# Both heads of a pair alternate on the two halves of the rows in the products inside the chunks of an RWKV-7 layer

## The chip, the cores and the metric

One core of a Trainium2 chip runs the whole kernel. The metric is device time in microseconds: the median of several runs of one program. Three runs of the kernel before are shown, and one more execution was profiled.

## What is computed

A diffusion-backbone layer over 2048 latent tokens with a context prefix of 256 tokens, width 1024, all in float32. After a modulated norm one projection feeds two groups of eight heads: attention in a 2-D neighbourhood, and RWKV-7 time mixing in both directions. Both are joined by an output projection, and a SwiGLU follows. The part that the change touches is the recurrence:

```python
# per direction and head, state S of 64 x 64, one step for each token
sa = einsum('bhvk,bhk->bhv', s, a_t)
s = s * w_t[:, :, None, :] + sa[..., None] * b_t[:, :, None, :] + v_t[..., None] * k_t[:, :, None, :]
y = einsum('bhvk,bhk->bhv', s, r_t)
# context tokens first (256), then the latent tokens (2048); forwards and backwards; 8 heads
```

## The kernel before

The program has three stages. `phase1` computes the norm, the input projection, and the decayed vectors of the recurrence, which it writes to the tensor `d_b`. `phase2` runs the recurrence and the attention beside each other. `phase4` makes the output projection and the SwiGLU.

The recurrence is computed in chunks of 64 tokens. There are 18 steps `s` (2 of the context and 16 of the latent tokens, 128 tokens each, so 2 chunks per step), 4 pairs of heads `hp` and 2 directions. In `phase2` it is made of four kinds of streams:

- `build(s, hp, w)`, 72 times (lines 965 to 1011): the products inside a step's chunks, for one pair of heads. For each of the pair's two heads `h` it multiplies, for four (direction, chunk) indices `j`, a 64x128 block of `bk` by a 64x128 block of `u.ga` (64x64 for the two steps of the context). Head 0's operands stand in partitions 0 to 63, head 1's in 64 to 127, so a product uses half of the rows of TensorE's array. Each head has a PSUM bank of its own, taken when its turn comes: four matmuls on line 996, then two ACT copies of the triangular part into `lx` (line 1002; one for each half of 32 rows, into columns that the inversion wants), a masked DVE product into `ga` (line 1004) and another into `gb` (line 1008), then the bank goes back.
- `inverses()`, 9 times, each for two steps (lines 1036 to 1111): the inverse of the triangular matrices `lx`. DVE transposes (line 1047), POOL masks, DVE solves 32x32 blocks by some 30 operations on the tile `lu` (lines 1061 to 1074), transposes back (lines 1077 and 1079), and small matmuls on lines 1094 and 1103 make the off-diagonal blocks, with copies between (1099, 1107).
- `lates(g)`: transposes of `bk` for the state's update (line 1029). It takes a bank too.
- `chains(g)`, for two groups of two pairs: the recurrence over the 36 chunks, where each chunk needs the state of the chunk before. A chunk of one group is eight matmuls on each of lines 1174, 1182 and 1189 with copies between them, and the outputs on lines 1200 and 1203.

Beside them stand the attention's streams (`prepare`, two `head` streams, `products`): matmuls on lines 672, 751, 754, 759, 789, 791, 824 and 830.

Only two PSUM banks, `bank0` and `bank1`, are shared by builds, lates, inverses and the attention's `prepare`. A stream asks for one by `yield "get", z, 1` and gives it back by `put`. The builds of two steps write the buffer `lx`, of which there are two; so the builds of the last two steps wait until the chain has passed step 13, and the chain's last two steps (four chunks) wait for the ninth inverse, which waits for all eight of those builds.

The order of the program is made by `emit`: a planner that holds the streams as generators, with a cost for each piece (`yield "run", ("PE", 1.0)` and the like), and takes the stream that can start first by its costs. A scheduler of the framework then sets the final order on each engine's queue. Each queue is served in order. [...]

The lines of the build before that matter:

```python
for h in range(2):
    z = []
    yield "get", z, 1
    yield "run", ("PE", 1.0)
    gp = z[0].rearrange("p (j t) -> p j t", j=4)
    for j in range(4):
        nc.tensor.matmul(gp[:, j, 0:N], bk[H[h], j], u.ga[H[h], h:3:2 - h, j, :] if s > 1 else
                         u.ga[H[h], h, j, :], start=True, stop=True)
```

Of the kernel before, what the change touches and what calls it, by code (L numbers as in the profile page):

```python
# [3 lines left out]

# [1 line left out]

# [7 lines left out]
AF = mybir.ActivationFunctionType  # L14
# [28 lines left out]

class K:
    pass


def setup(k, ctx, tc, I):
# [857 lines left out]
def phase2(k):  # L906
# [3 lines left out]
    tc, nc, I = k.tc, k.nc, k.I  # L910
    with ExitStack() as ctx:
# [10 lines left out]
        H = (slice(0, 64), slice(64, 128))  # L922
# [30 lines left out]
        for i in range(NU):  # L953
            u = K()
# [10 lines left out]
        def build(s, hp, w):  # L965

            G, j0 = s // 2, 4 * (s % 2)
# [19 lines left out]


            N = 128 if s > 1 else 64
            for h in range(2):  # L990
                z = []
                yield "get", z, 1
                yield "run", ("PE", 1.0)
                gp = z[0].rearrange("p (j t) -> p j t", j=4)
                for j in range(4):
                    nc.tensor.matmul(gp[:, j, 0:N], bk[H[h], j], u.ga[H[h], h:3:2 - h, j, :] if s > 1 else  # L996
                                     u.ga[H[h], h, j, :], start=True, stop=True)
                yield "run", ("ACT", -0.43), ("DVE", -0.34)
                ko = H[1 - h]
                for i in range(2):  # L1000
                    p0 = slice(64 * h + 32 * i, 64 * h + 32 * i + 32)
                    nc.scalar.activation(lx[p0, hp, j0:j0 + 4, 0:64 - 32 * i], gp[p0, :, 32 * i:64], AF.Copy)
                dc = "p (d c) t -> p d c t"
                nc.vector.tensor_tensor(u.ga[ko, h].rearrange(dc, d=2), gp[ko, :, 0:64].rearrange(dc, d=2),
                                        maskS[ko, :, None, :].to_broadcast([64, 2, 2, 64]), op=ALU.mult)
                if s > 1:
                    yield "run", ("DVE", -0.34)
                    nc.vector.tensor_tensor(u.gb[:, h].rearrange(dc, d=2), gp[:, :, 64:128].rearrange(dc, d=2),  # L1008
                                            maskI[:, h, :, None, :].to_broadcast([P, 2, 2, 64]), op=ALU.mult)
                yield "put", z[0]  # L1010
            yield "post", ("built", s, hp)

        def lates(g):
# [22 lines left out]
        def inverses():  # L1036
# [3 lines left out]
            for s in range(NS // 2):  # L1040
                yield ("wait",) + tuple(("built", 2 * s + e, hp) for e in range(2) for hp in range(4))
                lx = LX[s]
                lu = lx.rearrange("p g j t -> p (g j) t")
                lv = lu[:, :, 0:32]
                x = cp.tile([P, 32, 32], F32, tag="lu", name="lu")
                yield "run", ("DVE", 1.2)
                nc.vector.transpose(x.rearrange("u s t -> u t s"), lv.rearrange("s u t -> s t u"))
# [654 lines left out]
```

## Time and profile before

| | |
|---|---|
| median of 3 runs | 3642.16 us (3630.34 to 3642.43) |
| the profiled execution | 3625.81 us, span 3624.1 us, mean granted clock 0.972 |
| PE busy (matmuls) | 3497.2 us, 96% of the span |
| DVE, ACT, POOL busy | 69%, 43%, 29% |
| recurrence and attention (`phase2`) on PE | 889 to 1998 us of the span |
| line 996 | 1152 records, 177.85 us of busy time |

The profiled execution is 16 us (0.45%) shorter than the median of the runs. Busy time counts a matmul from its start to its modelled end; the matmuls overlap in the array, so the time that one takes from the others is read from the distance between starts. The granted clock is the share of TensorE's full clock (2.4 GHz); 0.5 is its lower level, 1.2 GHz.

### The profile page before, as it was taken

How to read it: one execution, taken by the hardware profiler on the slowest of the kernel's cores; microseconds unless marked ns; L12 is line 12 of the kernel's file. 1: busy time of each engine (PE TensorE's matmuls, PEld its weight loads, DVE VectorE, ACT ScalarE, POOL GpSimd, SP SyncE). 2: the span in 40 equal slices, each digit the busy share in tenths (PEclk: the TensorE clock that was granted, in tenths of full speed). 3: DMA queues.
4: the chain of work that ended last, by engine and by line, in shares of the span. 5: the costliest groups of instructions: out<-in, count | busy, mean ns of one | idle time of the engine just before them, and what ended most of it. 6: DMA issues, size and time to landing. Idle time of an engine off the chain costs nothing. (4 is left out here: it accounts for less than half of the span.)

```text
span 3624.1 us, 67102 instructions
## 1 busy us (share of the span) xinstructions
PE 3497.2 (96%) x25330; PEld 2916.3 (80%) x25330; DVE 2505.1 (69%) x4780; ACT 1541.8 (43%) x3502; POOL 1060.5 (29%) x1011
## 2 busy tenths in 40 slices
PE   7899999999999999999999999999899999899999
PEld 5787878889667777767776787888799999799998
DVE  7758886772686666676785674344877778777776
ACT  4524343442555555455555444323433333333332
POOL 3425543552000000000010342333433334433332
PEclk9999999999899999999999999999999999999999
DMA  7546666555443343433434455333412222422222
GB/s 240 164 147 200 194 193 182 162 162 124 127 89 108 109 90 106 129 67 93 131 99 142 151 189 180 97 93 98 149 59 70 70 70 70 163 67 70 70 70 67
DMA packets 502339, 440.70 MB, mean 122 GB/s; under 512 B 106096, under 2 KB 424960, under 8 KB 502016
## 3 DMA queue, kind: packets, MB, share of 16 engines
q1 hardware_dynamic: 502016, 436.42, 41.3%
q8 instruction: 199, 3.26, 0.4%
q14 instruction: 124, 1.02, 0.1%
HBM read 328.54 MB, written 107.75 MB: 120 GB/s over the span
## 5 line engine op out<-in xcount | busy, mean ns | idle before, releaser
L1311 ACT ACTIVATE w<-raw 128x512 fp32r<-128x512 f32 x440 | 269.8, 627 | 496.1 <-PE acc L1600 186.9
L1520 PE MATMUL acc<-ua,w 128*128 128x384 f32 x2464 | 469.9, 336 | 6.9 <-POOL w L1312 3.3
L1600 PE MATMUL acc<-w,fh 128*128 128x512 f32 x1408 | 437.8, 396 | 19.5 <-ACT fh L1311 7.6
L1312 DVE TENSOR_TENSOR w<-raw,w 128x512 fp32r<-128x512 f32 x308 | 277.5, 904 | 247.4 <-ACT w L1311 122.7
L1520 PEld LDWEIGHTS acc<-ua,w 128*128 128x128 f32 x2464 | 433.2, 189 | 10.9 <-POOL w L1312 4.6
L209 PE MATMUL acc<-u,wh 128*128 128x512 f32 (+3 forms) x1120 | 347.1, 390 | 11.2 <-DVE sh L247 6.1
L1600 PEld LDWEIGHTS acc<-w,fh 128*128 128x128 f32 x1408 | 267.8, 191 | 80.4 <-ACT fh L1311 9.2
L493 PE MATMUL acc<-wt,u 128*128 128x256 f32 x2496 | 320.1, 287 | 4.8 <-DVE sh L247 2.2
L493 PEld LDWEIGHTS acc<-wt,u 128*128 128x128 f32 x2496 | 306.9, 193 | 12.0 <-issue 4.3
L1591 POOL TENSOR_TENSOR raw<-raw,gate 128x512 f32<-128x512 f32 x132 | 181.4, 1384 | 413.4 <-DMA raw<-in_w_dram 364.0
L1600 PE MATMUL acc<-w,fl 128*128 128x512 f32 x704 | 270.1, 393 | 0.0
L1312 POOL TENSOR_TENSOR w<-raw,w 128x512 fp32r<-128x512 f32 x132 | 185.8, 1408 | 275.3 <-PE acc L1520 59.1
L1520 PE MATMUL acc<-ux,w 128*128 128x384 f32 x1232 | 252.1, 335 | 0.6 <-DVE w L1312 0.4
L209 PEld LDWEIGHTS acc<-u,wh 128*128 128x128 f32 (+1 forms) x1120 | 205.8, 191 | 57.7 <-issue 10.8
L1502 PE MATMUL acc<-ua,w 128*128 128x512 f32 x1056 | 241.7, 389 | 2.3 <-POOL w L1312 1.4
L1502 PEld LDWEIGHTS acc<-ua,w 128*128 128x128 f32 x1056 | 198.0, 188 | 44.0 <-POOL w L1312 1.9
L209 PE MATMUL acc<-u,wl 128*128 128x512 f32 (+3 forms) x560 | 217.4, 388 | 3.6 <-DVE wl L200 3.5
L1520 PEld LDWEIGHTS acc<-ux,w 128*128 128x128 f32 x1232 | 216.7, 188 | 2.1 <-DVE w L1312 1.2
L1605 DVE TENSOR_TENSOR h<-h,acc 128x512 f32<-128x512 f32 x192 | 126.2, 682 | 99.6 <-PE acc L1600 99.2
L996 PE MATMUL bank<-ga,bk 64*128 64x128 f32 (+1 forms) x1152 | 177.8, 302 | 1.4 <-DVE gb L1008 0.6
L1512 DVE TENSOR_TENSOR t<-acc,t 128x384 f32<-128x384 f32 x308 | 169.4, 550 | 14.0 <-PE acc L1520 7.4
L1312 POOL TENSOR_TENSOR w<-s,w 128x512 fp32r<-128x512 f32 x88 | 130.7, 1486 | 149.6 <-PE acc L1520 59.2
(257 smaller groups left out, 7092.3 us busy)
## 6 DMA issues: line engine op xcount, KB each, us to landing
raw<-in_w_dram SPq DMA_DIRECT2D x132, 512.0 KB
raw<-in_w_dram SPq DMA_DIRECT2D x132, 256.0 KB
wada<-in_w_ada_dram SPq DMA_DIRECT2D x96, 256.0 KB
d_b<-bk SPq DMA_DIRECT2D x72, 256.0 KB
bkl<-d_b SPq DMA_DIRECT2D x144, 128.0 KB
bk<-d_b SPq DMA_DIRECT2D x72, 256.0 KB
d_b<-ar SPq DMA_DIRECT2D x136, 128.0 KB
xt<-in_x_dram SPq DMA_DIRECT2D x32, 512.0 KB
```

The source lines that it names most:

```text
L209: nc.tensor.matmul(acc[:m, :n], a_[:, kk % 4, :m], b_[b][:, kk, :], start=(i == 0), stop=(i == 23))
L493: nc.tensor.matmul(acc[:, 256 * e:256 * e + 256], a_[b][:, kk, (j + e) * P:(j + e + 1) * P], ws[kk][:, h, :], start=(i == 0), stop=(i == 23))
L996: nc.tensor.matmul(gp[:, j, 0:N], bk[H[h], j], u.ga[H[h], h:3:2 - h, j, :] if s > 1 else u.ga[H[h], h, j, :], start=True, stop=True)
L1311: nc.scalar.activation(hl[0], v, AF.Copy)
L1312: eng.tensor_tensor(hl[1], v, hl[0].bitcast(F32), op=sub)
L1502: nc.tensor.matmul(acc, hl[wi][:, kk, :], u[ui][:, 4 * hf + kk, :], start=q == 0, stop=q == 23)
L1512: vadd = lambda o, x, y: nc.vector.tensor_tensor(o, x, y, op=add)
L1520: nc.tensor.matmul(acc, w[wi][:, kk, :], u[i][ui][:, kk, :], start=q == 0, stop=q == 11)
L1591: nc.gpsimd.tensor_tensor(raw, raw, g2[:, o], op=ALU.mult)
L1600: nc.tensor.matmul(acc, a_[:, f, ts], w2[f][:, hl, :], start=(i == 0), stop=(i == 6 * np_ - 1))
L1605: nc.vector.tensor_tensor(hs[j][:, o], hs[j][:, o], acc, op=add)
```

## The change

Both heads of a pair now take their banks at the same time (`get` of 2), and the eight matmuls of a build are issued in the order head 0, head 1, head 0, head 1, over `j`. A small class chains them (`issue_after`), so that the scheduler keeps this order. The planner's cost of the matmuls is 1.0 once for both heads, where it was 1.0 for each. The two ACT copies of a head become one copy of 64 rows x 256 into `lx`, and the shift of the lower 32 rows by 32 columns, which the second copy had made, is now done by two POOL copies of 32 rows x 1024 at the head of each inverse. Each bank is given back when its own head's copies are planned.

```diff
+class Run:
+    def __init__(s, k):
+        s.k, s.last = k, None
+    def next(s):
+        return s.k.tc.issue_after(s.last) if s.last else nullcontext()
...
             N = 128 if s > 1 else 64
+            z = []
+            yield "get", z, 2
+            yield "run", ("PE", 1.0)
+            gp = [v.rearrange("p (j t) -> p j t", j=4) for v in z]
+            run = Run(k)
+            for j in range(4):
+                for h in range(2):
+                    with run.next():
+                        run.last = nc.tensor.matmul(gp[h][:, j, 0:N], bk[H[h], j], u.ga[H[h], h:3:2 - h, j, :] if s > 1
+                                                    else u.ga[H[h], h, j, :], start=True, stop=True).ins
+            dc = "p (d c) t -> p d c t"
             for h in range(2):
-                z = []
-                yield "get", z, 1
-                yield "run", ("PE", 1.0)
-                gp = z[0].rearrange("p (j t) -> p j t", j=4)
-                for j in range(4):
-                    nc.tensor.matmul(gp[:, j, 0:N], bk[H[h], j], u.ga[H[h], h:3:2 - h, j, :] if s > 1 else
-                                     u.ga[H[h], h, j, :], start=True, stop=True)
-                yield "run", ("ACT", -0.43), ("DVE", -0.34)
+                yield "run", ("ACT", -0.45), ("DVE", -0.34)
                 ko = H[1 - h]
-                for i in range(2):
-                    p0 = slice(64 * h + 32 * i, 64 * h + 32 * i + 32)
-                    nc.scalar.activation(lx[p0, hp, j0:j0 + 4, 0:64 - 32 * i], gp[p0, :, 32 * i:64], AF.Copy)
+                nc.scalar.activation(lx[H[h], hp, j0:j0 + 4, :], gp[h][H[h], :, 0:64], AF.Copy)
...
-                yield "put", z[0]
+                yield "put", z[h]
...
                 lv = lu[:, :, 0:32]
+                for h in range(2):
+                    p0 = slice(64 * h + 32, 64 * h + 64)
+                    nc.gpsimd.tensor_copy(lu[p0, :, 0:32], lu[p0, :, 32:64])
                 x = cp.tile([P, 32, 32], F32, tag="lu", name="lu")
```

How the order moves is seen at two places on PE's queue. The first is two builds of an early step, among the attention's matmuls (`sw`, `sx`, `po`), before:

```order
L996 MATMUL bank_9727<-ga_9773,bk 128x128 x4
L759 MATMUL sx<-kc,qz_9809 128x256
L789 MATMUL sx<-ident,pr 128x128 x2
L996 MATMUL bank_9728<-ga_9771,bk 128x128 x4
L791 MATMUL sw_9781<-ident,pr 128x128 x3
L830 MATMUL po<-ident,oT 128x128
L996 MATMUL bank_9727<-ga_9773,bk 128x128 x4
L751 MATMUL sw_9781<-ks,qz_9810 128x512
L754 MATMUL sw_9781<-mk 128x512
L824 MATMUL po<-pr,vc 64x128
L996 MATMUL bank_9728<-ga_9771,bk 128x128 x4
```

and one of these builds now (line 996 has become line 1008 of the new file):

```order
L1008 MATMUL bank_9727<-ga_9773,bk 128x128
L761 MATMUL sw_9781<-ks,qz_9810 128x512
L764 MATMUL sw_9781<-mk 128x512
L1008 MATMUL bank_9728<-ga_9773,bk 128x128
L1008 MATMUL bank_9727<-ga_9773,bk 128x128
L1008 MATMUL bank_9728<-ga_9773,bk 128x128
L1008 MATMUL bank_9727<-ga_9773,bk 128x128
L1008 MATMUL bank_9728<-ga_9773,bk 128x128
L1008 MATMUL bank_9727<-ga_9773,bk 128x128
L1008 MATMUL bank_9728<-ga_9773,bk 128x128
```

The build's two blocks of four have become one matmul, other work, and seven alternating ones. 52 of the 72 builds are cut in this way, after the first matmul, and 7 in another; 13 stand whole.

The second place is the ninth, last inverse (`bank<-x1t,lx` and `bank<-lx,fs`). Before, the rows around its first matmuls were these:

```order
L830 MATMUL po<-ident,oT 128x128
L1189 MATMUL pch_9729<-zv,tt 64x64 x2
L751 MATMUL sw_9781<-ks,qz_9808 128x512
L754 MATMUL sw_9781<-mk 128x512
L1094 MATMUL bank_9728<-x1t,lx 32x32 x32
L1094 MATMUL bank_9727<-x1t,lx 32x32 x32
L1182 MATMUL pch_9730<-rs,lx 64x64 x8
L1200 MATMUL pch_9729<-z_20374,ga_9767 64x64 x2
```

Now they are these (1275 and 1412 are `phase4`'s lines 1261 and 1398, 1108 and 1117 are the inverse's 1094 and 1103, 1196 and 1040 are 1182 of the chain and 1029 of the lates):

```order
L1008 MATMUL bank_9727<-ga_9755,bk 128x128
L1412 MATMUL mtp<-ident,mx 128x128 x4
L1275 MATMUL g<-gup,gd 128x512
L1412 MATMUL mtp<-ident,mx 128x128 x8
L1275 MATMUL g<-gup,gd 128x512 x3
L1108 MATMUL bank_9728<-x1t,lx 32x32 x32
L1108 MATMUL bank_9727<-x1t,lx 32x32 x32
L1117 MATMUL bank_9728<-lx,fs 32x32 x32
L1117 MATMUL bank_9727<-lx,fs 32x32 x32
L1196 MATMUL pch_9729<-rs,lx 64x64 x8
L1040 MATMUL bank_9728<-ident,bkl 128x128 x4
```

Attention stood on both sides of the last inverse; it no longer does. The attention's last matmul on PE (line 830 before) had 133 matmuls of `phase2` behind it, and now has 881. Those are, in the order now: 63 of the builds' (8 builds but one matmul), 120 on each of the chain's three lines (15 chunks of one group), 128 on each of the two lines of the outputs (16 such chunks), 44 of the lates' transposes, and the 128 of the last inverse; with 24 and 6 matmuls of `phase4` between them.

## Rows read from the trace of the kernel before

**Rows 1.** The page's first part: busy time of each engine, share of the span, instructions.

```profile
PE 3497.2 (96%) x25330; PEld 2916.3 (80%) x25330; DVE 2505.1 (69%) x4780; ACT 1541.8 (43%) x3502; POOL 1060.5 (29%) x1011
```

**Rows 2.** Stretches of the span: from and to, length, then busy time of PE, PEld, DVE, ACT and POOL (with instructions), the granted clock, the DMA's share and GB/s.

```profile
889.00:1970.00 1081.00, 1052.44 (x12037) 774.31 (x12036) 737.56 (x1863) 585.44 (x1638) 53.85 (x65) 0.95 0.41 106
1970.00:1998.00 28.00, 20.22 (x262) 15.18 (x260) 21.26 (x41) 9.98 (x22) 6.61 (x4) 0.76 0.76 203
1420.00:1466.00 46.00, 43.09 (x585) 35.88 (x584) 17.49 (x44) 19.36 (x49) 4.26 (x10) 0.67 0.31 89
1435.00:1466.00 31.00, 31.00 (x292) 26.13 (x286) 9.58 (x24) 10.70 (x28) 0.00 (x0) 0.50 0.22 65
```

**Rows 3.** The stretch of `phase2`, instructions of line 996 alone: busy time of PE and PEld, granted clock, DMA.

```profile
889.00:1998.00 1109.00, 177.85 (x1152) 148.94 (x1152) 0.94 0.42 108
```

**Rows 4.** PE's timeline: start and length in us, engine, line, operation, out<-in, shapes, records merged. A head's four matmuls and the row after them, then one matmul alone and the row after it.

```profile
1200.71 1.16 PE L996 MATMUL bank<-ga,bk 64*128 64x128 f32 x8
1201.80 0.91 PE L751 MATMUL sw<-ks,qz 128*128 128x384 f32 x2
...
1347.23 0.49 PE L996 MATMUL bank<-ga,bk 64*128 64x128 f32 x2
1347.64 1.13 PE L751 MATMUL sw<-ks,qz 128*128 128x512 f32 x2
```

**Rows 5.** PE's timeline at two more places. First the attention's products, whose two heads alternate on the two halves of the columns (22 records from 1331.76 to 1333.22), and behind them eight matmuls of two builds: four of a head 1 and four of a head 0, so of different halves of the rows. Then, at 1584, eight matmuls of two builds that are both of a head 0, so of the same half.

```profile
1331.76 0.54 PE L824 MATMUL po<-pr,vc 128*64 128x128 f32 x5
...
1333.22 1.71 PE L996 MATMUL bank<-ga,bk 64*128 64x128 f32 x16
1334.86 0.45 PE L1189 MATMUL pch<-zv,tt 128*64 128x64 f32 x6
...
1584.10 2.05 PE L996 MATMUL bank<-ga,bk 64*128 64x128 f32 x16
1586.08 0.33 PE L1182 MATMUL pch<-rs,lx 64*64 64x64 f32 x4
```

**Rows 6.** Who waited for whom on PE in 889 to 1998: engine, tile, line, what ended the wait; us in total, times, longest. The rows of line 996.

```profile
PE bank L996 <- DVE gb L1008: 0.6, 1, 0.6
PE bank L996 <- DVE ga L1004: 0.4, 1, 0.4
```

**Rows 7.** Groups of instructions by line and shape, in 889 to 1998 (the POOL row: of the whole span): busy us, mean ns of one, then idle time before them and what ended it.

```profile
L1002 ACT ACTIVATE lx<-bank 32x256 f32<-32x256 f32 x144 | 53.6, 373 | 116.2 <-PE bank L996 109.8 <-DVE z L1194 1.5 <-DVE z L1206 1.3
L1002 ACT ACTIVATE lx<-bank 32x128 f32<-32x128 f32 x144 | 38.7, 268 | 1.7
L1210 ACT COPY zv<-pch 64x256 f32<-64x256 f32 x128 | 46.7, 365 | 65.8 <-PE pch L1203 57.3 <-issue 4.9 <-DVE ot L834 2.2
L1004 DVE TENSOR_TENSOR ga<-bank,maskS 64x256 f32<-64x256 f32 x144 | 60.5, 420 | 151.4 <-ACT lx L1002 150.1
L329 POOL COPY sq<-rho 128x512 f32<-128x512 f32 x16 | 11.3, 706 | 0.6
```

**Rows 8.** PE's timeline near the end of `phase2`, at the full clock: two of the chain's pieces, `phase4`'s transposes, and the first and the last row of one chunk's outputs (lines 1200 and 1203, from 1970.65 to 1972.76).

```profile
1967.23 0.68 PE L1182 MATMUL pch<-rs,lx 64*64 64x64 f32 x16
1967.84 0.69 PE L1189 MATMUL pch<-zv,tt 128*64 128x64 f32 x16
...
1969.42 0.82 PE L1398 MATMUL mtp<-ident,mx 128*128 128x128 f32 x6
...
1970.65 0.33 PE L1200 MATMUL pch<-z,ga 64*64 64x64 f32 x4 [0.30 <-DVE z L1194]
...
1972.76 1.13 PE L1261 MATMUL g<-gup,gd 128*128 128x512 f32 x2
```

**Rows 9.** PE's timeline inside 1435 to 1466, where no attention stands on PE: the chain's pieces, a head of a build, an output piece, and the lates' transposes.

```profile
1436.02 1.12 PE L1189 MATMUL pch<-zv,tt 128*64 128x64 f32 x16
1437.07 0.47 PE L1182 MATMUL pch<-rs,lx 64*64 64x64 f32 x2
1437.48 2.07 PE L996 MATMUL bank<-ga,bk 64*128 64x128 f32 x8
...
1440.74 0.48 PE L1203 MATMUL pch<-zv,gb 128*64 128x64 f32 x4
...
1463.27 1.12 PE L1029 MATMUL bank<-ident,bkl 128*128 128x128 f32 x4
```

**Rows 10.** The last inverse on DVE: its first transpose, its last, and its last copy (timeline); then the busy time of DVE and POOL on the tile `lu` in that stretch, and the reductions, which write another tile.

```profile
1836.11 2.14 DVE L1047 STREAM_TRANSPOSE lu<-lx 128x1024 f32<-128x1024 f32 x1
...
1893.11 1.90 DVE L1079 STREAM_TRANSPOSE x1t<-lu 128x1024 f32<-128x1024 f32 x1
...
1911.24 0.69 DVE L1107 COPY lx<-bank 32x512 f32<-32x512 f32 x1
...
1836.00:1896.00 60.00, 24.37 (x30) 1.26 (x1) 1.00 0.45 123
...
L1073 DVE TENSOR_REDUCE red<-xtmp 128x112 f32<-128x448 f32 (+3 forms) x7 | 6.7, 951 | 0.1
```

More of the change, by code (lines that the diff above doesn't have):

```diff
@@ L2 @@
 import math
-from contextlib import ExitStack
+from contextlib import ExitStack, nullcontext
 import numpy as np
@@ L989, in build @@
             N = 128 if s > 1 else 64
-            for h in range(2):
-                z = []
-                yield "get", z, 1
-                yield "run", ("PE", 1.0)
-                gp = z[0].rearrange("p (j t) -> p j t", j=4)
-                for j in range(4):
-                    nc.tensor.matmul(gp[:, j, 0:N], bk[H[h], j], u.ga[H[h], h:3:2 - h, j, :] if s > 1 else
-                                     u.ga[H[h], h, j, :], start=True, stop=True)
-                yield "run", ("ACT", -0.43), ("DVE", -0.34)
-                ko = H[1 - h]
-                for i in range(2):
-                    p0 = slice(64 * h + 32 * i, 64 * h + 32 * i + 32)
-                    nc.scalar.activation(lx[p0, hp, j0:j0 + 4, 0:64 - 32 * i], gp[p0, :, 32 * i:64], AF.Copy)
-                dc = "p (d c) t -> p d c t"
-                nc.vector.tensor_tensor(u.ga[ko, h].rearrange(dc, d=2), gp[ko, :, 0:64].rearrange(dc, d=2),
+            z = []
[9 more added lines that the diff above has]
+            dc = "p (d c) t -> p d c t"
+            for h in range(2):
+                yield "run", ("ACT", -0.45), ("DVE", -0.34)
+                ko = H[1 - h]
+                nc.scalar.activation(lx[H[h], hp, j0:j0 + 4, :], gp[h][H[h], :, 0:64], AF.Copy)
+                nc.vector.tensor_tensor(u.ga[ko, h].rearrange(dc, d=2), gp[h][ko, :, 0:64].rearrange(dc, d=2),
                                         maskS[ko, :, None, :].to_broadcast([64, 2, 2, 64]), op=ALU.mult)
@@ L1007, in build @@
                     yield "run", ("DVE", -0.34)
-                    nc.vector.tensor_tensor(u.gb[:, h].rearrange(dc, d=2), gp[:, :, 64:128].rearrange(dc, d=2),
+                    nc.vector.tensor_tensor(u.gb[:, h].rearrange(dc, d=2), gp[h][:, :, 64:128].rearrange(dc, d=2),
                                             maskI[:, h, :, None, :].to_broadcast([P, 2, 2, 64]), op=ALU.mult)
-                yield "put", z[0]
+                yield "put", z[h]
             yield "post", ("built", s, hp)
```

## The prediction

> **What bounds the kernel now.** I read the page's busy shares first: PE is busy 96% of the span, the next engine, DVE, 69% [rows 1]. The change touches `phase2` alone, so I looked at its stretches next. From 889 to 1970 us, where recurrence and attention stand beside each other, PE is busy 1052 of 1081 us, DVE 738 and ACT 585 [rows 2]. So a microsecond taken from PE's queue counts there, as long as other work stands behind it. Two shorter stretches show the other regime: from 1970 to 1998, behind the attention's end, PE is busy 20 of 28 us at a granted clock of 0.76; and from 1435 to 1466, where only builds and chains stand on PE, the clock is at 0.5, the lower level of 1.2 GHz, all the time, though PE counts as busy for all 31 us [rows 2]. The reader is to see that PE without attention is both slower and emptier.
>
> **The matmuls of the builds.** Line 996 has 1152 records and 178 us of busy time [rows 3]; what it takes from the others is read from starts. A head's four matmuls (8 records) start at 1200.71 and the next row at 1201.80, so 1.09 us [rows 4]; 72 builds of two heads are 72 x 2.18 = 157 us. Do products on different halves of the rows run beside each other? The trace has places where two builds happen to meet. Sixteen records of the same half take 1584.10 to 1586.08, 1.98 us; sixteen of which eight are on the one half and eight on the other take 1.64 us, 1333.22 to 1334.86 [rows 5]. They were not even alternating, and only some of them overlapped where the blocks meet. A full alternation is seen in the attention's products, which alternate on halves of the columns: 22 records from 1331.76 to 1333.22, 0.066 us each [rows 5]. At that rate a whole build of 16 records takes 1.06 us. The order shows 13 builds whole, and 59 cut, nearly all into one matmul and seven. One alone takes 1347.23 to 1347.64, 0.41 us [rows 4], and 14 records at 0.066 take 0.93, so 1.34. The sum is 13 x 1.06 + 59 x 1.34 = 93 us, and **the gain 157 - 93 = 64 us**. Its lower end is the 1.64 us of the accidental meeting, with 0.2 us more for a cut: 157 - 72 x 1.64 - 59 x 0.2 = 27 us. Its upper end is half of the old time, 78 us. I take 64, since the alternating products are the row most like the new one.
>
> **What lies behind the attention's last matmul.** The gain is PE time, so the planner pulls the attention forward, and it ends early: 881 matmuls of `phase2`'s part of the queue stand behind it, where there were 133. The builds of the last two steps, the last inverse and the last chunks have no cover any more. Their work at the full clock: 45 chain pieces of 0.61 us (1967.23 to 1967.84), 27.5 us; outputs of 16 chunks of a group at 2.11 us (1970.65 to 1972.76), 33.8 us; 24 transposes of `phase4`, six of which last 0.82 us, 3 us, and 6 matmuls of 1.1 us, 7 us [rows 8]; 8 builds of 1.34 us, 11 us; 11 groups of the lates' transposes, 1.12 us at the lower clock [rows 9], so some 0.6, 7 us. Together 89 us, which must be done in either kernel. But at the lower clock a chain piece takes 1.05 us instead of 0.61 (1436.02 to 1437.07) and a head of a build lasts 2.07 us instead of 1.16 [rows 4, 9]: a factor of about 1.75. In the stretch from 1420 to 1466, 31 of 46 us were at the lower level [rows 2]; with the same two thirds, the 89 us cost **0.67 x 0.75 x 89 = 44 us more**. The ends are 0 (full clock) and 67 us (the lower level throughout).
>
> **What such stretches cost before** is given back: the 31 us at 0.5 did what takes 31 / 1.75 = 18 us, so 13 us; and 1970 to 1998 lost 8 us idle and some 6 us to the clock [rows 2]. **Minus 27 us**; the lower end is 14, if the order now has its own stretch like the first.
>
> **The last inverse.** It ran from 1836.11 to 1911.93, beside attention. Its operations on DVE are 24.4 us on the tile `lu` and 6.7 us of reductions, 31 us, and POOL's mask is 1.3 us [rows 10]. Added are the two POOL copies of 1024 columns. No row has that shape; a POOL copy of 512 takes 0.71 us [rows 7], so 1.3 us each, 2.6 us. From DVE's last transpose to the last copy it was 17 us beside other work [rows 10]; alone I take 7. That is 42 us in which the chain's last four chunks cannot start, and the order leaves PE a few pieces, 2 us, to do. So **PE stands nearly empty for 40 us**; the ends are 33 (the rest at 2 us) and 60 (DVE shares its time with `phase4`'s norms as it did with attention). In the first eight inverses the POOL copies have attention to cover them; without that cover they would cost 8 x 2.6 = 21 us. Behind them on POOL's queue stand the inverse's own mask and fills, and small copies of the attention's `prepare`, which has cover too.
>
> **Costed at nothing.** ACT saves two copies of 0.27 us and gains nothing much (373 ns for 32x256; a copy of 64x256 takes 365 [rows 7]): 72 x 0.55 = 39 us of an engine that is busy 585 of 1081 us. DVE waited 150 us for these copies [rows 7], and PE's work hid it. What is new is that a build takes both banks at once, so that lates, transposes and the inverse wait for its last mask product. PE waited 1.0 us in all at line 996 for DVE to free a bank [rows 6], so I take 0, with 15 us as the other end; a gain is excluded, as nobody gets a bank earlier.
>
> **The sum:** -64 + 44 - 27 + 40 = **-7 us**, on 3625.8 us of the profiled execution 3619 us. The median of the runs is 3642.2, 16 us above that execution, so the forecast is **3635 us**. A measurement of this kernel can tell about 0.5%, 18 us, from no change; this is no change.
>
> **The rivals.**
> - *The tail stays at the full clock.* The two groups' chains fill each other's waits, and the clock holds as it did in most of `phase2`. For it: the 28 us at the end had 0.76, not 0.5 [rows 2]. Against it: the 31 us at 0.5 were full of builds and chains. With 10 us instead of 44 and 38 for the inverse: -43 us, **3599 us**.
> - *The pairs halve the builds.* If cuts cost nothing and a pair takes the time of one, the gain is 78, the sum -21 us, **3621 us**. Against it: the lone matmul's 0.41 us [rows 4]. The Trainium skill (TensorEngine Tiling (Array Packing), Theoretical Speedup) gives up to 2x for a contraction of 64 rows or less; the trace agrees that halves overlap (1.64 against 1.98 us), but shows no doubling yet.
> - *The shared banks become the bound, slower than before.* At the end the eight builds and eleven groups of lates have the same two banks and nothing else to fill PE. A build then takes its matmuls at the lower clock (1.34 x 1.75 = 2.3 us), an ACT copy (0.37) and four mask products of 0.42 [rows 7], 4.4 us before the next can start, and a late with its copy some 1.7 us: 8 x 4.4 + 11 x 1.7 = 54 us, where I counted 18 us at the full clock, 27 with the lower one's share. If the chain's pieces don't fall into these gaps it costs 27 us: +20 us, **3662 us**. It decides from the point where PE waits over 3 us for a bank in each of these builds. For it: the order puts builds close behind each other there; against it: 1.0 us of such waits so far [rows 6]. The Trainium skill (TensorEngine Tiling (Array Packing), PSUM Bottleneck) says that tiling speeds the matmuls but not the emptying of PSUM, which may become the limit; no run here shows that yet.
> - *The halves don't overlap at all when they alternate.* Then the matmuls keep their 157 us and only the tail is new: -7 + 64 = +57 us, **3699 us**. Against it stand the 1.64 us of [rows 5].
>
> **How the numbers follow.** The forecast within 18 us has 0.44; the tail at the full clock 0.24 and the halved builds 0.07, both faster; the banks 0.20 and no overlap 0.05, both slower. So faster 0.31, same 0.44, slower 0.25. The range reaches from the tail at the full clock with some of the upper end of the gain, 3595, to the banks with a longer inverse, 3675. It leaves out the case without overlap and the far ends of the other two, under 0.2. The forecast alone spans 3624 to 3660.
>
> **What would show it.** In the changed profile a whole build should take 1.0 to 1.2 us from its first start to the next row, and its records come in pairs; the busy time of the builds should fall from 178 us to about 110. The attention's last row (830 before) should come some 150 us before `phase2`'s last, and between the last build and the last inverse's matmuls PE should be idle for some 35 us. The clock should show 0.5 in most of that tail. `phase4` should be unchanged. The forecast is wrong if the attention does not end early in time, if the tail holds the full clock, or if PE's waits for `bank` grow past 20 us.

## The result, and the profile after

The changed kernel takes **3663.55 us** (median of 4 runs, 3659.42 to 3665.99) against 3639.21 us for the kernel before on the same chip (median of 4). The ratio is 1.007, 95% interval 1.0055 to 1.0084: slower by 24 us. The forecast was 7 us faster, which it called no change. The time lies in the range given (3595 to 3675), the direction does not agree.

The line numbers of the changed file: the build's matmuls are 1008 (996 before), its ACT copy 1014 (two copies on 1002), its DVE products 1015 and 1019 (1004, 1008); the lates 1040 (1029); the new POOL copies 1058; the inverse's first and last transposes 1061 and 1093 (1047, 1079), its matmuls 1108 and 1117 (1094, 1103); the attention's last transposes 840 (830); `phase4`'s first ones 1275 and 1412 (1261, 1398). Each matmul leaves two records in the trace: line 1008 has 1152 records for 72 x 8 matmuls.

The page's first part, to be read against [rows 1]: PE is busy for 60 us less, and the span is 35 us longer.

```profile
PE 3437.3 (94%) x25330; PEld 2855.7 (78%) x25330; DVE 2505.8 (68%) x4780; ACT 1506.3 (41%) x3358; POOL 1082.6 (30%) x1029
```

The stretches of the changed kernel's `phase2`, as in [rows 2]: up to the attention's last matmul, then three parts of what is behind it, then all that is behind it, then the whole.

```profile
894.80:1862.40 967.60, 903.42 (x10593) 645.52 (x10591) 651.52 (x1722) 504.16 (x1389) 52.32 (x66) 0.95 0.41 103
1862.40:1920.00 57.60, 51.83 (x797) 40.19 (x794) 33.23 (x80) 27.14 (x67) 13.37 (x10) 1.00 0.59 171
1920.00:1990.00 70.00, 22.38 (x349) 15.19 (x348) 59.96 (x80) 8.76 (x17) 24.71 (x19) 0.54 0.19 58
1990.00:2034.60 44.60, 34.68 (x563) 27.13 (x557) 17.84 (x34) 20.55 (x44) 0.00 (x0) 0.81 0.64 178
1862.40:2034.60 172.20, 108.89 (x1698) 82.50 (x1695) 111.03 (x192) 56.45 (x127) 38.08 (x29) 0.76 0.44 127
894.80:2034.60 1139.80, 1012.31 (x12288) 728.02 (x12286) 762.55 (x1913) 560.61 (x1516) 90.40 (x95) 0.92 0.41 107
```

PE idle is length minus PE's busy time. Before, [rows 2] give 28.6 us up to the attention's end and 7.8 us behind it. Now it is 64.2 and 63.3 us. So `phase2` is 31 us longer: PE is busy for 60 us less and idle for 91 us more. `phase4` lasts 1625 us in both. The rest of the difference between the profiled executions, some 4 us, lies in `phase1`, which the change does not touch.

The builds. First line 1008 in the whole stretch ([rows 3] had 177.85 us); then from PE's timeline one whole build, a cut one's first matmul, and a cut one's other fourteen records, each with the row behind it (compare [rows 4, 5]).

```profile
894.80:2034.60 1139.80, 120.86 (x1152) 93.48 (x1152) 0.92 0.41 107
```

```profile
1172.73 1.16 PE L1008 MATMUL bank<-ga,bk 64*128 64x128 f32 x16
1173.82 0.44 PE L799 MATMUL sx<-ident,pr 128*128 128x128 f32 x2
...
1177.04 0.49 PE L1008 MATMUL bank<-ga,bk 64*128 64x128 f32 x2
1177.46 0.54 PE L834 MATMUL po<-pr,vc 128*64 128x128 f32 x5
...
1168.03 1.16 PE L1008 MATMUL bank<-ga,bk 64*128 64x128 f32 x14
1169.11 0.33 PE L840 MATMUL po<-ident,oT 128*128 128x128 f32 x1
```

A whole build takes 1.09 us where the two heads took 2.18. A cut one takes 0.42 + 1.08 = 1.50.

Waits on PE up to the attention's end (columns as in [rows 6]), the seven largest:

```profile
PE bank L1040 <- DMA bkl<-d_b: 8.4, 4, 4.3
PE sx L769 <- ACT pr L794: 6.7, 6, 2.5
PE sx L799 <- ACT pr L794: 6.6, 7, 2.4
PE bank L1108 <- DVE x1t L1093: 6.5, 4, 2.9
PE sw L761 <- ACT pr L804: 3.9, 8, 1.1
PE sw L801 <- ACT pr L795: 3.8, 8, 1.2
PE bank L682 <- DMA sg<-d_k: 2.7, 2, 2.1
```

All rows of this view that name `bank` add up to 31 us, where before they were 11; those of the attention's tiles `sx`, `sw` and `po` to 28, where they were 13. No single wait is large. The rows that name `bank` are waits of all matmuls that write a bank, whatever ended them. Of the 31 us only some 8 ended with a product or copy that empties a bank (lines 1014, 1015, 1019 and 1043), where before it was 1 to 2; 8.4 ended with a DMA of `bkl`, 8.6 with the inverse's or the attention's work on DVE ahead of line 1108.

The last inverse, which [rows 10] answer to, no longer has attention beside it. DVE's first and last transposes and the first of its last two copies:

```profile
1929.01 2.08 DVE L1061 STREAM_TRANSPOSE lu<-lx 128x1024 f32<-128x1024 f32 x1
...
1976.41 1.87 DVE L1093 STREAM_TRANSPOSE x1t<-lu 128x1024 f32<-128x1024 f32 x1
...
1984.32 0.69 DVE L1121 COPY lx<-bank 32x512 f32<-32x512 f32 x1 [0.92 <-ACT lx L1121]
```

PE in the same stretch; the bracket is PE's idle time ahead of the row and what ended it:

```profile
1919.07 1.13 PE L1008 MATMUL bank<-ga,bk 64*128 64x128 f32 x14 [0.24 <-DVE gb L1019]
1922.61 1.09 PE L1412 MATMUL mtp<-ident,mx 128*128 128x128 f32 x4 [2.42 <-DVE mx L1291]
...
1937.39 1.12 PE L1412 MATMUL mtp<-ident,mx 128*128 128x128 f32 x4 [11.13 <-DVE mx L1291]
...
1944.83 2.07 PE L1275 MATMUL g<-gup,gd 128*128 128x512 f32 x2 [4.61 <-DVE mx L1291]
1959.44 2.07 PE L1275 MATMUL g<-gup,gd 128*128 128x512 f32 x2 [12.55 <-DVE mx L1291]
1978.43 3.53 PE L1108 MATMUL bank<-x1t,lx 32*32 32x32 f32 x125 [16.91 <-DVE x1t L1093]
```

From the last build (1919) to the inverse's matmuls (1978) PE has a few pieces of `phase4`. Its waits for them, 31 us, end with norms on DVE, the last 17 us with the inverse. The norms share DVE with the inverse, whose tile `lu` and reductions take 27.3 and 6.7 of its 60 busy microseconds there.

The copies ([rows 7]), as groups by line with the mean ns of one:

```profile
L1014 ACT ACTIVATE lx<-bank 64x256 f32<-64x256 f32 x144 | 54.3, 377 | 44.4 <-PE bank L1008 40.1 <-DVE lu L1088 2.3
L1058 POOL COPY lx<-lx 32x1024 f32<-32x1024 f32 x18 | 21.4, 1191 | 441.3 <-ACT lx L1014 440.7
```

### The profile page after: what moved, and what is told of

Read it like the earlier page. It is cut to its first block, busy times and chain, and to the rows that moved or that the text cites. A ratio compares the mean times of both kernels' runs of the same rounds, so it can differ in the third digit from the quotient of the medians.

```text
span 3659.6 us, 66950 instructions
## 1 busy us (share of the span) xinstructions
PE 3437.3 (94%) x25330; PEld 2855.7 (78%) x25330; DVE 2505.8 (68%) x4780; ACT 1506.3 (41%) x3358; POOL 1082.6 (30%) x1029
## 3 DMA queue, kind: packets, MB, share of 16 engines
q14 instruction: 123, 1.01, 0.1%
## 5 line engine op out<-in xcount | busy, mean ns | idle before, releaser
L1454 PE MATMUL acc<-wo,mh 128*128 128x512 f32 x512 | 169.0, 404 | 0.9 <-ACT zv L1224 0.9
```

What stands on the lines that cost most here:

```text
L1454: nc.tensor.matmul(acc, a_[:, kk, :], ws[kk][:, hl, n * 512:(n + 1) * 512], start=(i == 0), stop=(i == 23))
```

## The experiments

The runs stand in four groups: attention due at 62, the two without alternation, and head 1 first; attention due at 63 and the section on copies and planner's numbers; both on one chip; then, on another, attention due at 61.5, norms behind, the pair at 2.0, and products twice; and the three on the same half. In each group the kernel before ran too (medians 3645.25, 3639.91, 3637.9 and 3638.59 us), and ratios are against it, with their 95% interval. Runs of different groups are compared by medians, and by ratios where these say something else by 5 us or more. Three theories stood at first. **Theory 1**: the attention ends too early, and the end without cover costs what the overlap gains. **Theory 2**: taking both banks at once makes PE wait. **Theory 3**: alternating halves gains little. Unless said otherwise an edit is made to the changed kernel.

### Is it the end without cover?

**Attention due later**: one number of the planner.

```diff
-LATE = (60, 60, 60, -10, -10, 0, 0, 0, 60, 60, 0)
+LATE = (60, 60, 60, -10, -10, 0, 0, 0, 62, 62, 0)
```

> The changed kernel with one number of the planner different: the due time of the two attention streams is 62 instead of 60, so that the recurrence goes ahead of them. In the order the attention's last matmul then has 104 matmuls of the recurrence behind it (the kernel before: 120, the changed one: 851), and the last inverse has attention on both sides again. Theory 1 (uncovered end): what lies behind the attention's last matmul took 172 us for 89 us of work, and this is where the forecast's gain went; with cover the excess of 83 us goes but for some 14 us, which the kernel before has too: 3664 - 69 = 3595, and anything up to 3615 fits. Theory 2 (shared banks): it is the banks, held as a pair, on which PE waits in the dense part (about 31 us on banks against 8 before); then the end's work only moves and waits elsewhere: 3640 to 3660. Theory 3 (the alternation gains little): near the kernel before, 3630 to 3645.

Measured: 3582.96 us, ratio 0.9828 (0.9803 to 0.9852), 62 us faster than before and 81 faster than the changed kernel (88 by the ratios). The stretches up to and behind the attention's end, and the whole:

```profile
892.70:1929.50 1036.80, 960.48 (x12058) 700.96 (x12056) 728.96 (x1868) 548.01 (x1499) 75.35 (x83) 0.95 0.43 110
1929.50:1953.80 24.30, 16.45 (x219) 11.52 (x219) 17.41 (x34) 8.31 (x18) 6.30 (x4) 0.81 0.79 216
892.70:1953.80 1061.10, 976.93 (x12276) 712.47 (x12273) 746.36 (x1901) 556.32 (x1515) 81.64 (x87) 0.94 0.44 113
```

Theory 1's number, and the best version here: it beats both kernels. But PE is still idle for 76 us ahead of the attention's end. This did not come back with the cover. Only some 8 us of it ended, as above, with a bank being emptied, so theory 2 covers little of it. (By all rows that name `bank` the kernel before waited 11 us, not the 8 of the expectation.)

**Attention due at 61.5**: `-60, 60` `+61.5, 61.5` in the same place.

> The changed kernel with attention due at 61.5: 660 matmuls of the recurrence behind the attention's last (851 at 60, 104 at 62), 24 instead of 63 of them matmuls of builds, still no attention beside the last inverse. Theory 1 (the price of the uncovered end is mostly the last inverse, 55 us of PE's 63 us idle): the price stays nearly whole, 3640 to 3660. Rival (it is the number of matmuls without cover, at the lower clock): 660 - 104 of 851 - 104 is three quarters of 81 us, so about 3643, and the granted clock behind the attention's end tells it: idle time there as in the changed kernel for theory 1, less lower clock for the rival.

Measured: 3634.48 us, ratio 0.9992 (0.9976 to 1.0007), 29 us faster than the changed kernel. The stretches up to and behind the attention's end:

```profile
896.10:1865.80 969.70, 904.71 (x10966) 652.66 (x10965) 665.49 (x1756) 513.71 (x1420) 54.85 (x66) 0.95 0.43 106
1865.80:2017.70 151.90, 92.21 (x1321) 68.58 (x1318) 99.47 (x157) 44.80 (x97) 41.75 (x29) 0.69 0.44 123
```

Both numbers are too high. Behind the attention's last matmul PE is idle for 59.7 of 151.9 us (63.3 of 172.2 in the changed kernel): this part stayed, as theory 1 says. PE's busy time there fell from 108.9 to 92.2 us, with fewer matmuls left: this is like the rival, but the rival's sign, less lower clock, did not come. The granted clock there is 0.69, in the changed kernel 0.76. Ahead of it PE is idle for 65.0 us, as in the changed kernel.

**Norms behind the last inverse.**

```diff
     def tile(s, y, j):
+        with s.k.tc.issue_after(s.k.inverted):
+            s.tile_(y, j)
+
+    def tile_(s, y, j):
```

Here `s.k.inverted` is the last inverse's transpose on line 1093, and `tile_` is what `tile` was.

> The changed kernel (attention due at 60, 851 to 881 matmuls behind its last), with the norms of phase4's first tiles put behind the last inverse's final transpose on DVE; PE's matmuls of these tiles then follow the inverse too. In the changed kernel DVE was busy 60 of the 70 us from 1920 to 1990, about half of it with these norms, and PE stood 63 us idle behind the attention's end. Theory 1 (the price of the uncovered end is the inverse's latency on a shared DVE): the inverse takes some 42 us alone instead of 57 and starts 3 to 8 us sooner; phase4's first tiles come later, beside the last chunks: 10 to 25 us faster, 3640 to 3653. Rival (the norms have to be done somewhere; PE then waits for them at phase4's start): 3655 to 3675.

Measured: 3652.41 us, ratio 1.0047 (1.0028 to 1.0065), 11 us less than the changed kernel by the medians; the two intervals overlap. DVE's first and last transposes, then PE's wait:

```profile
1922.81 2.08 DVE L1061 STREAM_TRANSPOSE lu<-lx 128x1024 f32<-128x1024 f32 x1 [0.73 <-POOL lx L1058]
...
1954.24 1.88 DVE L1093 STREAM_TRANSPOSE x1t<-lu 128x1024 f32<-128x1024 f32 x1
```

```profile
PE bank L1108 <- ACT lx L1098: 35.8, 1, 35.8
```

Between the starts of these transposes lie 31.4 us instead of 47.4: the norms had made the inverse 16 us longer. PE still waits 36 us in one piece, which is the inverse alone; behind the attention's end it is idle for 51 us instead of 63.

**The pair costs the planner 2.0**: `-("PE", 1.0)` `+("PE", 2.0)`.

> The changed kernel with one number of the planner different: the eight matmuls of a pair cost it 2.0, as the two heads together did before, instead of 1.0. The forecast said that the attention is pulled forward because the planner sees less PE time. In the order it still ends early (869 matmuls behind its last). So if the early end is from taking both banks at once: 3650 to 3675, as the changed kernel. If it is from the planner's cost: 3585 to 3615.

Measured: 3671.5 us, ratio 1.01 (1.0076 to 1.0124). The early end does not come from the planner seeing less PE time, as the prediction had it. Nor does it come from the alternation (823 matmuls of the recurrence stand behind the attention's end without it) or from the copies (128 with the copies alone). What is left of the change, beside the chaining and small numbers of the planner, is taking both banks at once; by this elimination it is the likely cause, not tried by itself.

**Attention due at 63.**

> The changed kernel with attention due at 63: a few of the attention's tiles now stand behind the recurrence's last matmul, and none of the recurrence behind the attention's. Theory 1 (an end of the recurrence without cover costs): the last 24 us of the run at 62 were the recurrence alone; they are covered now, but the last attention tiles stand alone: between 10 us faster and 10 us slower than 3583, so the optimum is flat here. If the cover of the recurrence's end were worth its whole length: 3560.

Measured: 3616.2 us, ratio 0.9938 (0.9914 to 0.9962), 33 us slower than at 62 (40 by the ratios). Neither number fits, and the optimum is not flat. The mean clocks of its six runs are 0.959 to 0.969, those at 62 are 0.969 to 0.973; the profiled execution, the slowest of the six, has 0.959.

### What is the alternation worth?

**Head 0 four times, then head 1 four times**, in the changed kernel and with attention due at 62:

```diff
-            for j in range(4):
-                for h in range(2):
+            for h in range(2):
+                for j in range(4):
```

> The changed kernel with its own due times (attention ends early: 823 matmuls of the recurrence behind its last), but the eight matmuls of a build go head 0 four times, then head 1 four times, with both banks taken together. It undoes the alternation alone. Theory 1: the tail stays and the gain goes: 3664 + 46 to 64 = 3710 to 3728. Theory 2 (shared banks): 3670 to 3690, since part of the builds' time is hidden in waits for banks. Theory 3 (the alternation gains little): 3655 to 3670.

Measured: 3669.71 us, ratio 1.0057 (1.0036 to 1.0079), no different from the changed kernel.

> As the run with attention due at 62, but the eight matmuls of a build go head 0 four times, then head 1 four times; both banks are still taken together, the copies are the new ones, and the order around them is nearly the same (104 matmuls behind the attention's last). Theory 1 (uncovered end, and the alternation gains what the rows show): 46 to 64 us slower than the same order with alternation, so 3640 to 3665. Theory 2 (shared banks): 10 to 30 us slower, as PE's time is hidden in waits for banks. Theory 3 (the alternation gains little): within 10 us of the alternating one.

Measured: 3592.89 us, ratio 0.9854 (0.9829 to 0.9878), 10 us slower than with alternation; the intervals overlap. Both agree with theory 3, although its builds take PE for 157 us, not 118. Either PE's time is worth little there, or the order that came with the edit hid the loss. Two more edits were made to tell.

**Each product twice**, due at 62: `-for j in range(4)` `+for j in (0, 1, 2, 3, 0, 1, 2, 3)`.

> The run with attention due at 62, with each build's eight alternating matmuls made twice (the second eight write the same values again). It adds 72 builds x 16 records x 0.066 us = 76 us of PE work at the full clock, to find what a microsecond of PE is worth there. Undoing the alternation added 29 us to the builds' share of the time and cost 10 us. If PE has slack in that stretch (83 us idle in it), the doubling costs 25 to 50 us: 3608 to 3633. If PE is the bound as the forecast assumed: 70 to 85 us, 3653 to 3668.

Measured: 3656.19 us, ratio 1.0055 (1.0035 to 1.0075), 73 us slower (83 by the ratios) for an estimated 76 us of work. An added microsecond of PE's work costs about one. By itself this would also fit a bound by the banks, which are held while the added matmuls run; but PE is busy for 960 of 1037 us ahead of the attention's end at 62, and waits some 8 us there for a bank to be emptied. So as far as these runs show PE is the bound there, and not the copies. The Trainium skill (TensorEngine Tiling (Array Packing), PSUM Bottleneck) says that the emptying of PSUM may become the limit after a fourfold speedup; this run does not show it.

**Both heads on the same half**, the order of every engine unchanged:

```diff
-    bk[H[h], j], u.ga[H[h], h:3:2 - h, j, :]
+    bk[H[0], j], u.ga[H[0], 0:3:2, j, :]
```

> The changed kernel, with the same order on every engine, instruction for instruction, and the same two banks; only head 1's eight records now read head 0's operands, so that both heads' matmuls use the same half of the rows and cannot overlap (head 1's products are so replaced by a second copy of head 0's, with the masks of head 0). It takes the overlap away and leaves the order. Sixteen records of one half took 1.98 us, sixteen alternating ones 1.09. Theory P (PE is the bound where the builds stand, and the small effect of undoing the alternation came from the other order that went with it): 72 x some 0.75 to 0.9 us = 54 to 65 us slower, 3718 to 3729, perhaps 5 less for the builds in the tail. Theory S (the alternation's time goes into waits for banks and for ACT's exponentials): 5 to 20 us slower, 3669 to 3684.

This kernel and the two after it leave out head 1's own products, so they do not compute the layer; they are read for their time alone.

Measured: 3696.24 us, ratio 1.0151 (1.0123 to 1.018), 33 us slower than the changed kernel by the medians, 29 by the ratios. A cut build's fourteen records and one whole build; then line 1008 alone in the whole stretch, the stretch up to the attention's end, and the whole stretch:

```profile
1173.00 1.83 PE L1008 MATMUL bank<-ga,bk 64*128 64x128 f32 x14
1174.75 0.33 PE L840 MATMUL po<-ident,oT 128*128 128x128 f32 x1
1178.37 2.05 PE L1008 MATMUL bank<-ga,bk 64*128 64x128 f32 x16
1180.35 0.44 PE L799 MATMUL sx<-ident,pr 128*128 128x128 f32 x2
```

```profile
898.30:2070.50 1172.20, 171.85 (x1152) 144.79 (x1152) 0.92 0.40 104
898.30:1893.10 994.80, 938.46 (x10592) 686.26 (x10592) 663.78 (x1722) 503.91 (x1390) 51.49 (x66) 0.96 0.40 100
898.30:2070.50 1172.20, 1056.67 (x12284) 777.88 (x12282) 777.03 (x1913) 560.26 (x1516) 90.08 (x95) 0.92 0.40 104
```

Without the overlap a whole build takes 1.98 us and fourteen records 1.75, with it 1.09 and 1.08. PE is busy for 44 us more and idle for 12 less.

The same with attention due at 62:

> The run with attention due at 62, with the same order on every engine, and head 1's records on head 0's half of the rows as in the run before this one (head 1's products are a second copy of head 0's). Theory P: 50 to 65 us slower than 3583, so 3633 to 3648. Theory S: 5 to 20 us, 3588 to 3603.

Measured: 3644.5 us, ratio 1.0009 (0.999 to 1.0028): 61 us slower than with the overlap (66 by the ratios), and no different from the kernel before.

```profile
890.00:2011.50 1121.50, 1050.35 (x12276) 782.22 (x12273) 758.92 (x1901) 556.66 (x1515) 79.93 (x87) 0.92 0.41 107
```

And in the head-major order:

> The run without alternation and with attention due at 62 (3593 us), same order, both heads on head 0's half of the rows (head 1's products are a second copy of head 0's). It tells what the head-major order owes to builds whose two heads meet: sixteen records 1.64 us against 1.98 of one half, in 26 builds that stand whole, and smaller meetings with other pieces. Theory P: 26 x 0.34 = 9 us and up to as much again from pieces of the chain, 3602 to 3612. Theory S: no difference, 3588 to 3598.

Measured: 3602.96 us, ratio 0.9899 (0.9876 to 0.9922), 10 us slower than its partner (16 by the ratios). Theory P holds in all three by sign, and by size but in the changed kernel's own order, where 33 us lie between the two theories. Theory 3 falls: at 62 the head-major kernel lost most of the overlap (10 of 61 us are left) and won an order that is better by some 40 us (3644.5 against 3602.96, neither with overlap). At 60 no such pair was run.

**Head 1 first**, whose bank comes free later, due at 62: `-for h in range(2):` `+for h in (1, 0):`.

> As the run with attention due at 62, but the alternation begins with head 1, whose bank is the one that comes free later. In the order 35 builds instead of 18 stand whole and 40 instead of 49 are cut after their first matmul. Theory 1: a cut costs 0.28 us (1.34 against 1.06), so 17 builds x 0.28 = 5 us faster than the run with head 0 first, at most 10. Theory 2 (shared banks): PE's waits for banks fall too, 10 to 25 us faster. Theory 3: no difference.

Measured: 3590.48 us, ratio 0.9852 (0.9827 to 0.9878), not told apart from head 0 first.

### Copies and planner's numbers

**The copies alone**, on the kernel before: one ACT copy a head, and the POOL copies.

```diff
-                for i in range(2):
-                    nc.scalar.activation(lx[p0, hp, j0:j0 + 4, 0:64 - 32 * i], gp[p0, :, 32 * i:64], AF.Copy)
+                nc.scalar.activation(lx[H[h], hp, j0:j0 + 4, :], gp[H[h], :, 0:64], AF.Copy)
```

> The kernel before with the new copies alone: one ACT copy of 64 rows a head in place of two, and the two POOL copies at the head of each inverse. Banks, products and due times are those of before, and the order behind the attention's last matmul is nearly the same (128 matmuls against 120). The run without alternation but with attention due at 62 was 52 us faster than the kernel before, so something other than the alternation gains. Theory A (the copies): DVE's mask products waited 150 us for the ACT copies, and these go; 30 to 55 us faster than before, 3590 to 3615. Theory B (the order that follows from taking both banks at once: the heads' products meet on different halves and the recurrence is spread otherwise): within 10 us of before, 3635 to 3655. Theory C (any order with other planner's numbers would do): as B.

Measured: 3655.31 us, ratio 1.0037 (1.002 to 1.0053), 13 us slower. The copies by themselves do not pay.

**The planner's numbers alone**, on the kernel before: `("PE", 0.5)` a head, attention due at 60.5.

> The kernel before with two numbers of the planner changed and no instruction: the matmuls of a head cost it 0.5 instead of 1.0 (as much for a pair as in the changed kernel), and attention is due at 60.5 instead of 60, which keeps the attention's end beside the recurrence's (16 matmuls behind its last). Theory C (the order that other numbers give is what gained): 3590 to 3615. Theories A and B: within 15 us of before, 3630 to 3660.

Measured: 3613.94 us, ratio 0.9926 (0.9904 to 0.9948), 27 us faster by the ratio without one changed instruction: an order alone moves that much, and theory C has its number.

```profile
897.20:1981.90 1084.70, 1038.52 (x12267) 766.10 (x12264) 744.01 (x1883) 594.20 (x1654) 53.33 (x65) 0.95 0.41 107
```

PE is idle for 46 us, 10 more than before, and busy for 33 us less with the same matmuls. By lines, most of this is the chain's: lines 1174, 1182, 1189, 1200 and 1203 together are busy for 360 us, where they were 392. Two of them, in the kernel before and then in this one:

```profile
L1203 PE MATMUL pch<-zv,gb 128*64 128x64 f32 x1024 | 99.9, 252 | 0.0
L1174 PE MATMUL pch<-zv,ga 128*64 128x64 f32 x1152 | 69.0, 237 | 1.2 <-DMA zv<-d_vs 0.6 <-ACT zv L1210 0.5
```

```profile
L1203 PE MATMUL pch<-zv,gb 128*64 128x64 f32 x1024 | 91.3, 246 | 0.0
L1174 PE MATMUL pch<-zv,ga 128*64 128x64 f32 x1152 | 61.1, 233 | 1.0 <-DMA zv<-d_vs 0.5 <-ACT zv L1210 0.4
```

**The old copies with the alternation**, due at 62.

> The changed kernel with attention due at 62, and the old copies: two ACT copies a head, no POOL copies. Both banks are taken together and the halves alternate. In the order 96 matmuls stand behind the attention's last. Against the 3583 us of the same kernel with the new copies: theory A (the copies gain): 25 to 50 us slower, 3608 to 3633. Theory B (the order of the pair): 3578 to 3593. Theory D (the POOL copies delay the inverses): faster, 3560 to 3575.

Measured: 3602.96 us, ratio 0.9896 (0.9874 to 0.9917), 20 us slower than with the new ones, short of theory A's numbers (25 by the ratios, their lower end). Here the new copies gain, alone they lose.

## Why the prediction was wrong, point by point

**The step that failed is PE's idle time. The sum has 40 us of it at the last inverse and, in what it costed at nothing, none ahead of the attention's end; the profile has 63 behind that end and 36 more than before ahead of it.** The gain of the builds failed too as a gain of time: the forecast took 64 us, and in the changed kernel the overlap is worth 33 (29 by the ratios).

The two profiled executions can be set against the sum term by term. The idle times are read; the split of PE's busy time in `phase2` into work and clock is an estimate from the granted clock in slices of 4 us: the time at the lower level is twice the clock's shortfall from 1, and busy time at that level counts as 1 / 1.75 of it at the full clock, the prediction's own factor.

| term | forecast | in the profiles |
|---|---|---|
| gain of the builds | -64 | -46, the overlap's work by the run on the same half |
| work saved without the overlap | not in the sum | -17 |
| lower clock behind the attention's end | +44 | +14 |
| given back | -27 | -19 |
| PE idle behind the attention's end | +40 | +63 |
| PE idle ahead of it | 0 | +36 |
| sum | -7 | +31, the growth of `phase2` |

So PE's work fell by 63 us, nearly the forecast's 64, but by luck: 17 of them are there without the overlap as well, most of it in the chain's lines (392 us of busy time before, 361 in the run on the same half). By luck, too, the run on the same half meets the prediction's case without overlap (3699 us forecast, 3696 measured): the terms beside the gain were to give +57 and give +58 against 3638.59 us in that group. But in its profiled execution they are 79 us more idle time and 17 us less work, with 1 us more for the lower clock.

**The gain.** Fourteen alternating records take 1.08 us and not the 0.93 that the rate of the attention's products gave; 59 x 0.15 is 9 us. By blocks the overlap is 13 x (1.98 - 1.09) + 59 x (1.75 - 1.08) = 51 us, and line 1008's busy time falls by just that (171.85 to 120.86 us). Of these 51, PE's busy time in all keeps 44, and 12 more come back as idle time. With the attention's end in its place the same overlap is worth 61 us; PE's busy time falls by 73 there and idle time rises by 13. The difference between the two is the clock: by the same estimate PE was busy at the lower level for 120 us without and 125 with the overlap in the changed order, and for 152 and 98 with attention due at 62. That is 2 us lost in the one and 23 gained in the other; the work saved is alike, 46 and 50 us. Each is one profiled execution. Why the clock follows the overlap in one order and not in the other, no run tells.

**The tail** lasted 172 us; 89, 44 and 40 had made 173. The sum is right by luck and its making is not. The 44 us for the lower clock did not come. From 1862 to 1920, with builds and chains close behind each other, the clock was 1.00. It was at 0.54 from 1920 to 1990, where PE was busy only 22 of 70 us: most of the lower clock fell on time that PE spent idle, and by the estimate it cost 14 us. So the sign that the clock shows 0.5 in most of the tail is not met. The rival with the full clock, which put 10 us there, was nearer, though the mean clock of the tail was 0.76. In its place stands idle time: 5.8, 47.6 and 9.9 us in the three parts, of which 40 were forecast.

**The last inverse**, 40 us with the ends 33 and 60, took 47.6 us of PE's time. The far end's mechanism, DVE shared with `phase4`'s norms, is at work: with the norms behind, the inverse is 16 us shorter, and PE is idle for 12 us less behind the attention's end.

**Given back, -27 us**, came in part: the old end went with its 8 us idle and some 5 us of lower clock, but the lower clock ahead of the attention's end costs only 6 us less than before, not 13 (mean clock 0.95 in both). PE's idle time there rose from 28.6 to 64.2 us.

**Costed at nothing**, with 15 us as the other end: waits at rows that name `bank` rose by 20 us, waits of the attention's products for ACT and DVE by 14, which the prediction does not have at all. The sign it gave, waits for `bank` past 20 us, is met by the rows' name and not by its reason: waits for a bank to be emptied rose by some 6 us. The run on the same half is idle for 56.3 us ahead of the attention's end, so most of the rise comes without the overlap; which part of the new order makes it stays open. The POOL copies had cover; 1.19 us each is near the estimate of 1.3, and ACT's 377 ns near that of 365.

**The reason for the early end** was wrong: with the pair at 2.0 in the planner the attention ends as early. **The price of that end** was near in size: undoing it gains 81 us with the overlap (3663.55 to 3582.96), where 44 + 40 had been put down; but 77 in the head-major order (3669.71 to 3592.89) and only 52 on the same half (3696.24 to 3644.5), and it is idle time more than clock.

**The rivals.** Halved builds: a whole one is 1.98 to 1.09, a factor of 1.8; the Trainium skill (TensorEngine Tiling (Array Packing), Theoretical Speedup) gives up to 2x, which the trace approaches without a cut. The banks as the bound, at 3662 us, is the nearest number and not the cause: at the last builds, behind the attention's end, PE waits 1.6 us at line 1008 in all, not 3 in each.

What stays open: why orders of the same work differ by 27 to 42 us. By the estimate it is mostly the lower clock between 63 and 62 (PE busy at the lower level for 181 and 98 us) and between alternating and head-major without overlap at 62 (152 and 82). With the planner's numbers alone it is neither idle time nor mainly the clock, but the shorter busy time of the chain's lines. Nothing here tells which detail of an order sets these.

## What to carry to other kernels

Where a planner writes the order, a change of a resource request (here two banks at once) moves work across the whole stage; read from the order what is left behind the end of the covering work, and mend the due times before judging the change. The same edit of the instructions cost 24 us with one number of the planner and gained 62 with another. When the total is known, split it into work, clock and idle time before calling a term right: here the total behind the attention's end came out at 172 for 173 with each part off. To price an edit, keep the order and take away the one effect: removing the alternation by another loop order said 10 us at most, removing the overlap in the same order said 33 and 61.

## What the runs showed of the hardware

Matmuls of 64 rows on alternating halves, in two banks, take 1.09 us for sixteen records against 1.98 on one half; a lone first matmul costs 0.42 us, and the other fourteen records then take 1.08, nearly as long as all sixteen. Head-major, two blocks of eight records on different halves take 1.64 us. The mean granted clock over the span of the profiled executions lay between 0.959 and 0.975 among these kernels, whose edits hardly touch `phase1` and `phase4`.
